# Reordering the first loads, pairing weight pieces in one buffer, and moving transposes at a stage seam, in a two-layer hybrid decoder trunk

## The chip, the cores and the metric

The kernel runs on one core of one Trainium2 chip. The metric is the device time of one execution in microseconds (us). PE is the matrix engine, DVE the vector engine, ACT the scalar (activation) engine, POOL the general-purpose engine; SP issues the DMA transfers. Every engine works through its own queue in order.

## The reference

Two layers over a sequence of 1024 tokens with 1024 features, float32. Each layer, cut to what matters:

```python
h = rms_norm(x, pre_mix_norm)
z = h @ w_in                       # 1024 -> 2*512 (conv) + 3*512 (q, k, v)
u = c_a * sigmoid(c_g)             # gated linear unit, 512 channels
u = silu(layer_norm(causal_dwconv(u, conv_w, conv_b)))      # 31 taps
q, k = partial_rope(zq), partial_rope(zk)                   # 4 heads, two 64-wide halves each
o = (softmax(q1 k1^T) - lam * softmax(q2 k2^T)) @ v         # causal
o = rms_norm(o, subln_g) * (1 - lam_init)
x = x + rms_norm(concat(u, o) @ w_out, post_mix_norm)
h = rms_norm(x, pre_ffn_norm)
up = causal_dwconv(h @ w_up, ffn_conv_w, ffn_conv_b)        # 1024 -> 2*2816, 3 taps
x = x + rms_norm((gelu(g) * val) @ w_down, post_ffn_norm)   # 2816 -> 1024
```

## The kernel before

**Precision and weights.** Every float32 operand of a matmul is split in two parts, hi and lo: ACT copies it into the reduced format (hi) and DVE or POOL subtracts to get the rest (lo). Each product is three matmuls, lo times lo being left out. A weight comes from DRAM into a tile `raw` (a ring of `RAW = 4` tiles of 1024 columns), is split into `wh..`/`wl..` tiles, and the raw tile is then free. In the mixing stage `load` cuts each weight into pieces of 512 columns (convolution weights, tag w) or 384 columns (query, key and value weights, tag q); each piece takes a whole raw tile. `split` does the ACT copy (L463) and the subtraction on POOL or DVE (L469). Tag w has two slots, tag q four.

**Start of layer 0.** Eight tiles of 128 tokens, here called t0 to t7, are loaded by `first_x` and normalised by `prenorm`: ACT squares and sums (L357), DVE scales the sum (L347), POOL takes the power -0.5 (L349), DVE multiplies (L359, the tile is then normalised in place), PE transposes eight blocks (L364) in two groups of four, ACT copies the hi part (L366) and DVE subtracts for lo (L367). The transposes of t4 to t7 are tied behind given products by `anchors`: with `CB[0] = (9, 0, 1, 2)` those of t4 are free, t5 follows the first convolution product (`pg`), t6 the second (`pa`), t7 the first product of queries, keys and values (`pq`). The raw tiles of the first convolution weights may be split only after the fourth power on POOL (`pows[3]`), those of the first q weights only after the eighth (`pows[7]`). Tiles for x come from two tags with two buffers each, "y" and "xr"; the order `("y", "y", "xr")[t % 3]` puts t0, t1, t3, t4, t6 and t7 in y. Before the loop the kernel also loads the causal mask `nmask` (cast on DVE at L262), `cos` and `sin`; behind it `params(0)` loads the convolution taps `cw`, `cvec`, `subg` and the lambda vectors and prepares them on DVE.

**Order of the mixing stage.** A planner, `Flow`, runs at build time over generators with assumed costs and due times; it writes out the order on PE, DVE, ACT and POOL (`manual_schedule`). It takes a raw ring slot with `R["raw"].get()` and assumes that a load takes `W_LAT = 3.0`. What is outside of the planner's blocks (the eight `prenorm`s, all SP transfers) is placed by the compiler's list scheduler. PE's fill is `c00 q00 c01 ...`: convolution product `pg` (gate) and `pa`, then four `pq` products of one head, and so on.

**The seam to the feed-forward stage.** Products of the up-projection are numbered by slots in `seq`; each slot is 12 matmuls of 128x512. The first sixteen slots compute two products for each of eight column tiles ahead: `(e1,1) (e1,4) (e2,1) (e2,4) (e1,7) ...`, where e2 adds into the PSUM tile `px` that e1 began, after `e_copy` (ACT, L1462) has copied e1's result out. Tokens t4 to t7 of the normalised input `xn` (L1185) are transposed here by `norm_t` (L1357) ahead of slots `NORM_T = (2, 5, 8, 11)`; `norm_c` then forms four sums of them on DVE and ACT at that slot and the three behind it. Slot 17 is the first that needs the sums (`t2`).

Of the kernel before, what the change touches and what calls it, by code (L numbers as in the profile page):

```python
# [9 lines left out]
F32 = mybir.dt.float32  # L10
# [42 lines left out]
P_AHEAD = 3  # L53
NORM_T = (2, 5, 8, 11)
ACC_BUFS = 3
# [158 lines left out]
def build(tc, ap, out):  # L214
# [7 lines left out]
    with ExitStack() as top:  # L222
# [17 lines left out]
        def load_x(src, tag="xr"):  # L240
            t = xs.tile([P, YW if tag == "y" else D], F32, tag=tag, name="xr", bufs=2 if tag == "y" else XR)[:, 0:D]
            sy.dma_start(t, src)
            return t
# [6 lines left out]
        xin = [ap["x"][t * P:(t + 1) * P, :] for t in range(8)]  # L250
        first_x = lambda t: load_x(xin[t], ("y", "y", "xr")[t % 3])
        x0 = [first_x(0)]
# [4 lines left out]
        g_pre = gvec(0, 0)  # L257
        x0 += [first_x(1), first_x(2)]
        nmask = xs.tile([P, P], F32, tag="m0", name="nmask", bufs=4)
        sy.dma_start(nmask, ap["nmask"])  # L260
        nmaskr = const("nmaskr", [P, P], mybir.dt.bfloat16)
        ve.tensor_copy(nmaskr, nmask)  # L262
        cos = const("cosT", [P, 8, 8])
        sy.dma_start(cos, ap["cos"])
        sin = const("sinT", [P, 8, 8])
        sy.dma_start(sin, ap["sin"])
        negh = const("negh", [P, 8])
        ve.memset(negh, -0.5)

        def params(l):  # L270
# [5 lines left out]

            cw, cv, sg = ptile("cw", [P, 4, CK]), ptile("cv", [P, 3, 4]), ptile("sg", [P, 1])
            sy.dma_start(cw, ap["cw"][l])
            sy.dma_start(cv, ap["cvec"][l])
            sy.dma_start(sg, ap["subg"][l])  # L280
            lv = par.tile([P, 4, HD], F32, tag="lv", name="lv", bufs=1)
            sy.dma_start(lv, ap["lamv"][l:l + 1].broadcast_to([P, 4, HD]))
            cws, hv, ls, nl = ptile("cws", [P, 4, (CK + 1) // 2]), ptile("hv", [P, 2, 4]), ptile("ls", [P, 2]), ptile("nl", [P, 1])
            pars[l] = dict(cw=cw, cws=cws, cv=cv, hv=hv, sg=sg, nl=nl)
            yield
# [128 lines left out]
        for l in range(DEPTH):  # L414
            xres = xin if l == 0 else x2[l - 1]
            with ExitStack() as st:
# [4 lines left out]
                if l == 0:  # L421
                    for t in range(8):
                        late[t] = prenorm(ptr, x0[t] if t < 3 else first_x(t), g_pre, hh[t // 4], t % 4)
                if l == 0:
                    for _ in params(0):
                        pass
                p = pars[l]
# [16 lines left out]
                def load(key, src, n, tag, gate=None):  # L444
# [8 lines left out]
                    W[key] = hi, lo, wi  # L453
                    step = n if n <= HB else n // 2
                    for j in range(n // step):
                        ri = yield from R["raw"].get()
                        raw = rw.tile([P, 1024], F32, tag="raw", name="raw", bufs=RAW)
                        s = slice(j * step, (j + 1) * step)
                        sy.dma_start(raw[:, :step], src[:, s])
                        fl.spawn(split(key, j, raw[:, :step], hi[:, s], lo[:, s], step, ri, gate), fl.now + W_LAT)  # L460

                def split(key, j, raw, hi, lo, n, ri, gate):
# [7 lines left out]
                    t = fl.op("dve", dv(n), t) if vec else fl.op("pool", 0.1 + n / 470, t)  # L470
                    R["raw"].free(ri, t)
                    fl.set("W", key, j)
# [797 lines left out]
                def next_params():  # L1270
                    g = params(l + 1)
                    yield 200.0
                    next(g)
                    yield 220.0
                    next(g, None)
                    fl.op("dve", 1.6)

                if l + 1 < DEPTH:
                    fl.spawn(next_params())
# [582 lines left out]
```

## Time and profile before

| what | us |
|---|---|
| median of 3 runs | 2315.07 |
| lowest, highest | 2315.03, 2316.55 |
| profiled execution, its own time | 2314.21 |
| span of its profile (first to last instruction) | 2312.4 |
| PE busy in the span | 2202.4 (95%) |
| DVE, ACT, POOL busy | 1879.3, 1126.7, 832.6 |
| mean granted TensorE clock | 0.979 of full speed |

The profiled execution is 0.9 us shorter than the median, and 1.8 us of its time lie outside of the span. A granted clock of 1.00 is 2.4 GHz and 0.5 is 1.2 GHz; a stretch with a clock between them was at the lower level for part of it. Times in rows count from the span's start.

### The profile page before, as it was taken

What the parts mean: (1) busy time and instruction counts of PE and PEld (TensorE: products, weight loads), DVE (VectorE), ACT (ScalarE), POOL (GpSimd) and SP (SyncE); (2) the same over time, 40 slices, a digit from 0 to 9 for tenths busy, and PEclk for the clock granted to TensorE, in tenths of its full rate; (3) what the DMA queues carried; (4) which work ended last, traced back from release to release, by engine and by line L of the source; (5) the groups of instructions that cost most, each with busy time, mean ns of one, the idle gap of its engine ahead of it and who ended that gap; (6) DMA issues with size and microseconds to landing.
All of it is one profiled execution on the core that took longest, in us unless ns stands there. A gap on an engine that the chain in (4) does not pass through costs nothing. (4 is left out here: it accounts for less than half of the span.)

```text
span 2312.4 us, 31516 instructions
## 1 busy us (share of the span) xinstructions
PE 2202.4 (95%) x10568; PEld 1838.5 (80%) x10568; DVE 1879.3 (81%) x3287; ACT 1126.7 (49%) x2458; POOL 832.6 (36%) x894
## 2 busy tenths in 40 slices
PE   6999997999999999999889999979999999999998
PEld 5898895878877878788778988868788778787886
DVE  6988988667888888777889889896678888887777
ACT  4445456655444444444534545465554444445443
POOL 3324312245444545201533333122454554442024
PEclk9999997999999999999999999979999999999999
DMA  4313323454333343933433123235533343348353
GB/s 156 86 48 92 79 72 123 164 206 138 119 120 130 111 137 130 316 96 111 135 100 103 41 82 97 73 114 191 194 118 124 119 136 123 104 168 274 96 164 118
DMA packets 140129, 295.39 MB, mean 128 GB/s; under 512 B 16832, under 2 KB 33984, under 8 KB 139456
## 3 DMA queue, kind: packets, MB, share of 16 engines
q1 hardware_dynamic: 139968, 293.39, 39.7%
q8 instruction: 83, 1.36, 0.3%
q14 instruction: 78, 0.64, 0.1%
HBM read 198.44 MB, written 78.12 MB: 120 GB/s over the span
## 5 line engine op out<-in xcount | busy, mean ns | idle before, releaser
L1660 PE MATMUL pd<-wp,wo 128*128 128x512 f32 x1776 | 414.2, 395 | 4.8 <-DVE wp L1305 2.8
L1660 PEld LDWEIGHTS pd<-wp,wo 128*128 128x128 f32 x1776 | 333.9, 188 | 81.7 <-DVE wp L1305 3.6
L1609 PE MATMUL py<-t,wo 128*128 128x512 f32 x1584 | 381.8, 394 | 5.8 <-DVE cg L1477 5.8
L1609 PEld LDWEIGHTS py<-t,wo 128*128 128x128 f32 x1584 | 296.8, 188 | 77.4 <-ACT wo L1304 9.0
L1305 POOL TENSOR_TENSOR wo<-ws,wo 128x512 fp32r<-128x512 f32 x176 | 249.9, 1432 | 279.5 <-ACT wo L1304 274.1
L1609 PE MATMUL px<-hA,wo 128*128 128x512 f32 x1056 | 255.3, 394 | 0.0
L1305 POOL TENSOR_TENSOR wo<-raw,wo 128x512 fp32r<-128x512 f32 x132 | 181.4, 1378 | 166.1 <-ACT wo L1304 157.3
L1609 PEld LDWEIGHTS px<-hA,wo 128*128 128x128 f32 x1056 | 198.6, 189 | 44.5 <-ACT ea L1464 0.5
L1305 POOL TENSOR_TENSOR wo<-fa,wo 128x512 fp32r<-128x512 f32 x66 | 103.1, 1577 | 323.0 <-ACT wo L1304 293.9
L1304 ACT ACTIVATE wo<-ws 128x512 fp32r<-128x512 f32 x176 | 108.8, 627 | 136.7 <-PE py L1609 47.4
L1495 DVE SCALAR_TENSOR_TENSOR acc<-cg,fw,acc 128x512 f32<-128x512 f32 x176 | 132.6, 754 | 41.7 <-ACT acc L1483 38.1
L597 DVE SCALAR_TENSOR_TENSOR scr<-u,cw,scr 128x256 f32<-128x256 f32 (+2 forms) x288 | 158.0, 565 | 3.7 <-ACT scr L591 3.6
L852 ACT ACTIVATE e<-S,mxv 128x512 f32<-128x512 f32 (+2 forms) x192 | 110.1, 581 | 64.6 <-DVE mxv L847 41.2
L1483 ACT ACTIVATE acc<-cg,fb,fw 128x512 f32<-128x512 f32 x88 | 68.2, 774 | 148.8 <-DVE cg L1477 148.8
L857 POOL TENSOR_TENSOR sm<-sm 128x1 f32<-128x1 f32 x64 | 25.5, 398 | 316.9 <-ACT e L852 301.6
L499 PE MATMUL pq<-whq,hA 128*128 128x384 f32 x512 | 135.5, 346 | 3.9 <-ACT whq L463 3.9
L499 PE MATMUL pq<-whq,hB 128*128 128x384 f32 x512 | 133.9, 342 | 0.0
L1609 PE MATMUL pz<-b,wo 128*128 128x512 f32 x528 | 129.8, 394 | 1.9 <-DVE cv L1477 1.9
L1609 PE MATMUL pz<-t,wo 128*128 128x512 f32 x528 | 128.7, 392 | 0.0
L1609 PEld LDWEIGHTS pz<-b,wo 128*128 128x128 f32 x528 | 98.4, 188 | 27.4 <-issue 5.1
L843 DVE TENSOR_REDUCE mxv<-S 128x1 f32<-128x512 f32 (+2 forms) x192 | 100.5, 549 | 24.1 <-PE S L827 18.2
L1609 PEld LDWEIGHTS pz<-t,wo 128*128 128x128 f32 x528 | 99.1, 188 | 22.7
(279 smaller groups left out, 5027.2 us busy)
## 6 DMA issues: line engine op xcount, KB each, us to landing
raw<-in_wupd SPq DMA_DIRECT2D x104, 512.0 KB, 3.6
fa<-f SPq DMA_DIRECT2D x154, 256.0 KB, 2.7
f<-fs SPq DMA_DIRECT2D x88, 256.0 KB, 3.3
raw<-in_wmix SPq DMA_DIRECT2D x80, 256.0 KB, 3.0
f<-gg SPq DMA_DIRECT2D x66, 256.0 KB, 2.0
raw<-in_wmix SPq DMA_DIRECT2D x64, 192.0 KB, 2.4
qs<-sth SPq DMA_DIRECT2D x64, 128.0 KB, 2.4
os<-onT SPq DMA_DIRECT2D x16, 512.0 KB, 3.2
```

Source lines behind the costliest of these rows:

```text
L499: mm = pe.matmul(dst, a, b, start=first and k + j == 0, stop=final and k == n - 1 and j == 2)
L597: ve.scalar_tensor_tensor(dst, src, wk, dst, op0=ALU.mult, op1=ALU.add)
L843: ve.tensor_reduce(mv_[:, j:j + 1], S, axis=AX.X, op=ALU.max, negate=True)
L852: se.activation(e[:, c0:c0 + w], S, AF.Exp, bias=mv_[:, 0:1], accum_out=sm[:, j:j + 1])
L857: po.tensor_tensor(sm[:, 0:1], sm[:, 0:1], sm[:, 1:2], op=ALU.add)
L1304: se.activation(w[:, 0], raw, AF.Copy)
L1305: eng.tensor_tensor(w[:, 1], raw, f32(w[:, 0]), op=ALU.subtract)
L1483: se.activation(acc[n, v, hf], C[n][v][:, 2 + hf * HB:2 + hf * HB + HB], AF.Identity, bias=fb[:, mt:mt + 1], scale=fw[:, mt, 2:3])
L1495: ve.scalar_tensor_tensor(dst, c[:, j + hf * HB:j + hf * HB + HB], fw[:, mt, j:j + 1], a, op0=ALU.mult, op1=ALU.add)
L1609: pe.matmul(ps, x, y, start=first and k + j == 0, stop=k == 3 and j == 2, skip_group_check=not first)
L1660: pe.matmul(ps[tt], x, y, start=first and k + n == 0, stop=k == K2 - 1 and n == 2, skip_group_check=not first)
```

## The change

Three edits. The start: the first four tiles of x (was three) are loaded ahead, over tags y, y, xr, xr in turn, and nothing but the identity and the norm's gain goes among them; `nmask`, `cos`, `sin` and the parameters of layer 0 are loaded by a task of the planner at its time 1.0, and the mask's cast and the parameters' preparation on DVE come at its time 7.0. `nmask` gets a tile of its own. The raw ring: one raw tile now takes all pieces of a weight, so the four tiles hold eight pieces; it is freed when the last piece is split. The seam: the transposes come ahead of slots 4, 6, 9 and 12.

```diff
-NORM_T = (2, 5, 8, 11)
+NORM_T = (4, 6, 9, 12)
...
-        first_x = lambda t: load_x(xin[t], ("y", "y", "xr")[t % 3])
+        first_x = lambda t: load_x(xin[t], ("y", "y", "xr", "xr")[t % 4])
         x0 = [first_x(0)]
...
         g_pre = gvec(0, 0)
-        x0 += [first_x(1), first_x(2)]
-        nmask = xs.tile([P, P], F32, tag="m0", name="nmask", bufs=4)
-        sy.dma_start(nmask, ap["nmask"])
+        x0 += [first_x(1), first_x(2), first_x(3)]
+        nmask = const("nmask", [P, P])
         nmaskr = const("nmaskr", [P, P], mybir.dt.bfloat16)
-        ve.tensor_copy(nmaskr, nmask)
         cos = const("cosT", [P, 8, 8])
-        sy.dma_start(cos, ap["cos"])
         sin = const("sinT", [P, 8, 8])
-        sy.dma_start(sin, ap["sin"])
...
             cw, cv, sg = ptile("cw", [P, 4, CK]), ptile("cv", [P, 3, 4]), ptile("sg", [P, 1])
+            lv = par.tile([P, 4, HD], F32, tag="lv", name="lv", bufs=1)
+            cws, hv, ls, nl = ptile("cws", [P, 4, (CK + 1) // 2]), ptile("hv", [P, 2, 4]), ptile("ls", [P, 2]), ptile("nl", [P, 1])
+            pars[l] = dict(cw=cw, cws=cws, cv=cv, hv=hv, sg=sg, nl=nl)
+            yield
             sy.dma_start(cw, ap["cw"][l])
             sy.dma_start(cv, ap["cvec"][l])
             sy.dma_start(sg, ap["subg"][l])
-            lv = par.tile([P, 4, HD], F32, tag="lv", name="lv", bufs=1)
             sy.dma_start(lv, ap["lamv"][l:l + 1].broadcast_to([P, 4, HD]))
-            cws, hv, ls, nl = ptile("cws", [P, 4, (CK + 1) // 2]), ptile("hv", [P, 2, 4]), ptile("ls", [P, 2]), ptile("nl", [P, 1])
-            pars[l] = dict(cw=cw, cws=cws, cv=cv, hv=hv, sg=sg, nl=nl)
             yield
...
-                        late[t] = prenorm(ptr, x0[t] if t < 3 else first_x(t), g_pre, hh[t // 4], t % 4)
+                        late[t] = prenorm(ptr, x0[t] if t < 4 else first_x(t), g_pre, hh[t // 4], t % 4)
                 if l == 0:
-                    for _ in params(0):
-                        pass
+                    par0 = params(0)
+                    next(par0)
...
                     step = n if n <= HB else n // 2
+                    ri = yield from R["raw"].get()
+                    raw = rw.tile([P, 1024], F32, tag="raw", name="raw", bufs=RAW)
                     for j in range(n // step):
-                        ri = yield from R["raw"].get()
-                        raw = rw.tile([P, 1024], F32, tag="raw", name="raw", bufs=RAW)
                         s = slice(j * step, (j + 1) * step)
-                        sy.dma_start(raw[:, :step], src[:, s])
-                        fl.spawn(split(key, j, raw[:, :step], hi[:, s], lo[:, s], step, ri, gate), fl.now + W_LAT)
+                        sy.dma_start(raw[:, s], src[:, s])
+                        fl.spawn(split(key, j, raw[:, s], hi[:, s], lo[:, s], step, ri if s.stop == n else None, gate), fl.now + W_LAT)
...
-                    R["raw"].free(ri, t)
+                    if ri is not None:
+                        R["raw"].free(ri, t)
...
                     yield 200.0
                     next(g)
+                    next(g)
                     yield 220.0
...
+                def constants():
+                    yield 1.0
+                    next(par0)
+                    sy.dma_start(cos, ap["cos"])
+                    sy.dma_start(sin, ap["sin"])
+                    sy.dma_start(nmask, ap["nmask"])
+                    yield 7.0
+                    next(par0, None)
+                    ve.tensor_copy(nmaskr, nmask)
+                    fl.op("dve", 1.8)
+
+                if l == 0:
+                    fl.spawn(constants())
```

## Rows read from the trace of the kernel before

**Rows 1.** The page: busy time of the engines, share of the span of 2312.4 us, and instructions.

```profile
PE 2202.4 (95%) x10568; PEld 1838.5 (80%) x10568; DVE 1879.3 (81%) x3287; ACT 1126.7 (49%) x2458; POOL 832.6 (36%) x894
```

**Rows 2.** Busy time by stretch: from and to, its length, then busy us and instructions of PE, PEld, DVE, ACT and POOL, the granted clock, the DMA share and GB/s.

```profile
340.00:410.00 70.00, 53.39 (x272) 43.31 (x270) 60.03 (x152) 41.33 (x117) 16.72 (x32) 0.83 0.40 121
1485.00:1555.00 70.00, 53.25 (x268) 42.38 (x267) 61.69 (x155) 40.90 (x117) 17.53 (x35) 0.78 0.35 105
```

**Rows 3.** The start in order of time: start, length, engine, line, operation, count, and in brackets the idle time of the engine before it with what ended it.

```profile
9.89 1.06 ACT L357 ACTIVATE sqj<-xr 128x1024 bf16<-128x1024 f32 x1 [4.44 <-DMA xr<-in_x]
11.16 1.06 ACT L357 ACTIVATE sqj<-xr 128x1024 bf16<-128x1024 f32 x1
11.37 0.23 DVE L262 CAST nmaskr<-nmask 128x128 bf16<-128x128 f32 x1 [6.62 <-DMA nmask<-in_nmask]
12.39 1.28 DVE L359 SCALAR_TENSOR_TENSOR xr<-xr,rs,gb 128x1024 f32<-128x1024 f32 x1 [0.73 <-POOL rs L349]
13.73 1.97 PE L364 MATMUL pt<-ident,xr 128*128 128x128 f32 x8 [13.73 <-DVE ss L347]
18.34 1.97 PE L364 MATMUL pt<-ident,xr 128*128 128x128 f32 x8 [2.65 <-DVE hA L367]
20.87 1.82 PE L364 MATMUL pt<-ident,xr 128*128 128x128 f32 x8 [0.56 <-DVE hA L367]
21.15 1.04 ACT L357 ACTIVATE sqj<-xr 128x1024 bf16<-128x1024 f32 x1
25.13 1.67 PE L364 MATMUL pt<-ident,xr 128*128 128x128 f32 x8 [2.44 <-DVE hA L367]
26.79 0.79 PE L499 MATMUL pg<-hA,whw 128*128 128x512 f32 x1
```

**Rows 4.** An issue of SP at the start; then one row of the list of issues (the last number is us from issue to landing), and one of what SP waited for up to 60 us (total, times, longest).

```profile
1.65 0.42 SPq L247 DMA_DIRECT2D gb<-in_norms  x1
gb<-in_norms SPq DMA_DIRECT2D x1, 512.0 KB, 6.9
SPq L459 <- POOL wlq L469: 14.6, 8, 6.9
```

**Rows 5.** The first product of q weights (PE from 43.48) and what feeds it, in order of time.

```profile
38.60 3.94 POOL L469 TENSOR_TENSOR wlq<-raw,whq 128x384 fp32r<-128x384 f32 x4 [1.23 <-ACT whq L463]
43.48 0.59 PE L499 MATMUL pq<-whq,hA 128*128 128x384 f32 x2
45.72 4.45 POOL L469 TENSOR_TENSOR wlq<-raw,whq 128x384 fp32r<-128x384 f32 x4 [3.17 <-ACT whq L463]
50.51 1.04 PE L364 MATMUL pt<-ident,xr 128*128 128x128 f32 x8
51.30 0.59 PE L499 MATMUL pq<-whq,hA 128*128 128x384 f32 x2
53.56 0.27 DVE L691 TENSOR_TENSOR v<-pq,v 128x128 fp32r<-128x128 f32 x1
55.54 0.51 PE L499 MATMUL pq<-whq,hA 128*128 128x384 f32 x2
```

**Rows 6.** A normalisation on DVE beside a split on POOL.

```profile
31.00 1.27 POOL L469 TENSOR_TENSOR wlw<-raw,whw 128x512 fp32r<-128x512 f32 x1
31.07 2.29 DVE L359 SCALAR_TENSOR_TENSOR xr<-xr,rs,gb 128x1024 f32<-128x1024 f32 x1 [2.07 <-POOL rs L349]
```

**Rows 7.** The same place at the start of layer 1.

```profile
1172.88 0.75 DVE L396 SCALAR_TENSOR_TENSOR y<-m0d,rs,xr 128x512 f32<-128x512 f32 x1 [1.68 <-POOL rs L349]
1179.69 0.59 PE L499 MATMUL pq<-whq,hA 128*128 128x384 f32 x2
1188.86 1.01 PE L499 MATMUL pq<-whq,hA 128*128 128x384 f32 x2 [3.92 <-ACT whq L463]
1190.25 1.46 DVE L396 SCALAR_TENSOR_TENSOR y<-m0d,rs,xr 128x512 f32<-128x512 f32 x1 [0.92 <-POOL wlq L469]
1194.52 1.91 PE L364 MATMUL pt<-ident,xr 128*128 128x128 f32 x8
1197.71 1.28 DVE L359 SCALAR_TENSOR_TENSOR xr<-y,rs,gb 128x1024 f32<-128x1024 f32 x1
1200.60 1.04 PE L364 MATMUL pt<-ident,xr 128*128 128x128 f32 x8
```

**Rows 8.** The seam of layer 0 in order of time; the last row is a stretch, as in rows 2.

```profile
505.77 1.28 DVE L1185 SCALAR_TENSOR_TENSOR xn<-xe,rs,gb 128x1024 f32<-128x1024 f32 x1
505.88 1.06 ACT L1178 ACTIVATE xn<-xe 128x1024 f32<-128x1024 f32 x1 [0.23 <-DVE ss L347]
506.94 0.58 ACT L1462 ACTIVATE ea<-px 128x512 f32<-128x512 f32 x1
507.19 1.94 PE L1357 MATMUL pt<-ident,xn 128*128 128x128 f32 x8 [3.88 <-DVE ss L347]
546.27 4.69 DVE L1372 TENSOR_TENSOR t<-ts,t 128x512 fp32r<-128x512 f32 x4
553.71 2.96 PE L1609 MATMUL py<-t,wo 128*128 128x512 f32 x12
500.00:520.00 20.00, 16.12 (x73) 13.31 (x72) 18.95 (x29) 13.35 (x25) 13.08 (x11) 0.91 0.71 257
```

**Rows 9.** The longest run of splits on POOL in the middle of the mixing stage of layer 0.

```profile
180.71 4.22 POOL L469 TENSOR_TENSOR wlq<-raw,whq 128x384 fp32r<-128x384 f32 x4
```

## The prediction

> **What bounds the kernel now.** I read the page first. PE is busy for 2202.4 of 2312.4 us [rows 1], so almost all of the time is matrix work that this change leaves alone; what it can win or lose lies in the 110 us in which PE stands, and in the time that PE works at its lower clock behind such a stand. The view by stretches says where these are. The two tails of the mixing stages, 70 us each, hold 16.6 and 16.8 us of standing, at a mean clock of 0.83 and 0.78 [rows 2]. Then I read PE's timeline for every gap over 0.3 us and the timelines of the engines that end them. The reader is to see three places outside of the tails. At the start PE's first transposes come at 13.73 and the first product at 26.79 [rows 3]. The first q product takes 7.0 us where the next takes 4.2 [rows 5], and its counterpart in layer 1 takes 14.8 [rows 7]. At the seam PE stands for 3.88 us ahead of the transposes [rows 8].
>
> **The start.** The first square on ACT is done long before DVE may scale it: the mask's cast stands ahead in DVE's queue and waits until 11.37, and 6.62 us of DVE's idle time end there. The first normalisation runs at 12.39 [rows 3]. Without the cast the next thing late is the gain: issued at 1.65, 6.9 us to landing, so 8.55 [rows 4]. The first normalisation may then run at about 8.7, which is 3.7 earlier, and the transposes at 10.0.
>
> Next is DVE's chain of four tiles. The fourth tile was late too (its square at 21.15), since its transfer waited for the transposes of the first. Now it is fourth in the queue and has a free buffer. The squares of the second and third tile began at 9.89 and 11.16 [rows 3]; one step more puts the fourth at about 12.4, and it binds no longer. Spacing of tiles on PE: 18.34 to 20.87 is 2.5 us with nothing late; 13.73 to 20.87 over two tiles is 3.6, but with the mask's successors, the parameters' small DVE instructions, between them [rows 3]. The last transposes would begin at 17.5 by the first and at 20.7 by the second. The first product came 1.66 behind them (25.13 to 26.79), so at 19.2 or 22.4 where it was at 26.79: a gain of 4.4 to 7.6. I take 5.5, near the middle, for splits on POOL now run beside this chain. A normalisation beside one took 2.29, against 1.28 [rows 3, 6].
>
> That row meets a rule that speaks against the change. The Trainium skill, page "SBUF — State Buffer", section "Who interferes with whom", says that a DVE instruction with two SBUF inputs and a GpSimd instruction that reads SBUF exclude each other, and that the later one waits out the earlier. The trace agrees here: 1.01 us of a 1.27 us split were added. If all four splits of the first weights met a normalisation, the rule would make the start up to 4 us worse and the sum below -5.4.
>
> The q product: its eight splits run in two groups, 38.60 to 42.5 and 45.72 to 50.2, and PE follows the second piece by piece [rows 5]. The second group is late because its raw tiles came free late: SP waited 14.6 us for these splits [rows 4]. With eight pieces in the ring, four of the eight are loaded at once and the rest as soon as the first convolution weights are split; in the planner's order all eight then come ahead of the convolution taps on ACT. The gate, the eighth power on POOL, comes with the tiles. The eight need 3.94 + 4.45 = 8.4 us on POOL and PE reaches them two products behind the start, so the 7.0 falls towards 4.2: a gain of 0 to 2.8. But DVE is full there. It frees the first product's PSUM bank at 53.8, and PE takes it again at 55.54 [rows 5], a slack of 1.7. DVE's lead stays at 5.5, so PE may gain 5.5 + 1.7 = 7.2 in all. Start: **-7.2**, bounds -4.4 and -10.4.
>
> The moved transfers (nmask, cos, sin and the four parameters, seven issues on SP) queue behind the first raw pieces and among the late x tiles, for whose buffers SP stands in its queue until PE has transposed the tile before. What needs them is late: the taps follow the second product, rope and the mask come later still. I cost them at nothing. If the order on DVE puts the preparation ahead of a late x tile, DVE waits for them as it now waits for the mask.
>
> **Layer 1.** The q product loses 14.8 - 4.2 = 10.6, from ACT's split standing behind taps that wait for DVE (3.92 of idle time) and from late pieces [rows 7]. The ring removes both. What is late next is DVE's chain for the last token tile: normalised at 1197.71, transposed at 1200.60. Its additions take 1.46 beside POOL's q splits (1190.25), where the same one of an earlier tile took 0.75 (1172.88); two tiles of two additions each run so, and with the q splits done before, 4 x 0.7 = 3 us come back. PE then waits for the transposes rather than for weights. Bounds 0 (the chain keeps its time) and -10.6; I take the chain: **-3.0**.
>
> **The seam.** PE stands until 507.19 because the first tile is normalised at 507.05. Moved two slots on, the transposes are not waited for. But slot 2, which PE reaches instead, adds into the bank that `e_copy` must have read, and that copy stands on ACT behind the four squares of the same normalisations: it runs from 506.94 to 507.52 [rows 8]. PE stands until about 507.6, then does the same work in another order. Slot 17 begins at 553.71, and DVE ends the sums of the last tile at 551.0 [rows 8], the one that slot 17 needs first among them: 2.7 us of cover for sums that start later, 0 if PE gains as much. So the stall only changes its name: +0.4 per layer, **+0.8** in all. The bounds: if ACT's order lets the copy run when its product is done, 3.88 goes, and with it the lower clock behind it. The stretch 500 to 520 has 0.91 [rows 8], that is 3.6 us at 1.2 GHz or 1.8 lost; 2 x 5.7 = -11.4. On the other side +3 if the sums come late.
>
> **The order of the rest.** The planner sees other load times and writes another order for 2 x 350 us of mixing. PE waits for no weights there now, so no gain is due; the tails, with 16 us of waits each [rows 2], can fall either way. I take 0, bounds -5 and +5.
>
> **Sum.** -7.2 - 3.0 + 0.8 + 0 = -9.4. Against the profiled 2314.2 that is 2304.8; the median lies 0.9 above it, so **2305.7**.
>
> **The rivals.**
> *The seam's stall does go.* For it: ACT idles between the squares, so an order with the copy among them exists. Against: nothing in the edit touches that order, and layer 1 has the same one. Time: the +0.8 becomes -11.4, so 2293.5.
> *The lead is eaten.* Constants that DVE waits for, splits beside normalisations, or taps on a DVE that is full leave only some 3 us of the start and nothing in layer 1, or the tails cost 5 more. For it: the start goes through DVE's queue tile by tile, and each of these would stand in that queue. Time: -3 to -4.4 + 0.8, so about 2312.
> *POOL's queue (slower).* A ring of eight pieces lets a whole q weight, eight splits, follow one another. The longest run in mid-stage is four, 4.22 us [rows 9]; eight would take 8.4, and the sums of the softmax, which POOL does between the exponentials and their combination, wait up to 4.2 more. There are three further q weights a layer, six places: 25 us if all is exposed on PE, so 2331. It decides (2319.7 and above) from (9.4 + 4.6) / 6 = 2.3 us exposed at each. Against: the four q slots come free one after another, so the loads stay spread, and PE has other products to fill with.
>
> **How the numbers follow.** 0.2% is 4.6 us; less than that a measurement of this kernel can't tell from no change. My sum, with 2299 to 2310.4 as its own range: 0.57. The seam's stall gone: 0.14. The lead eaten: 0.19. POOL's queue or another loss beyond 0.2%: 0.10. Faster takes the first two and a little of the third: 0.73; same 0.17; slower 0.10. The range takes in the second case and the third with the bounds of the terms that they share with mine, 2290 to 2316; it leaves out the slower case and the outer tenths of those two, some 0.17.
>
> **What would show it.** Right: DVE's first normalisation at 8.5 to 9, the first product at 19 to 22.5, the first q product about 4.2 us long, with its splits ahead of the taps; in layer 1 no wait for whq, and PE waiting for a normalisation instead; at the seam PE standing until 507.6 less the lead, released by the copy of L1462, with the transposes behind two products. Wrong: the copy ahead of the squares on ACT, or the first product still behind 24, or longer waits of PE in the tails than 16 us, released by POOL or by DVE's combination.

## The result: no gain, and a profile that gives the start's lead back

| | before | after |
|---|---|---|
| median, 16 runs each, same chip | 2315.05 | 2319.36 |
| lowest, highest | 2313.18, 2322.36 | 2317.21, 2321.33 |
| span of the profiled execution | 2312.4 | 2317.6 |

The ratio is 1.0016, with a 95% interval of 1.0009 to 1.0024: slower by 0.16%, which is within the 0.2% below which I said that a measurement can't tell it from no change. The forecast was 2305.7 with 0.73 for faster, and 2319.4 lies outside of its range of 2290 to 2316.

PE's busy time on the page of after, and the two tails by stretch (columns as in [rows 2]):

```profile
PE 2199.5 (95%) x10568; PEld 1837.2 (79%) x10568; DVE 1878.3 (81%) x3285; ACT 1127.9 (49%) x2458; POOL 831.0 (36%) x896
...
340.00:410.00 70.00, 54.36 (x276) 42.90 (x275) 63.36 (x161) 42.44 (x121) 19.68 (x35) 0.83 0.42 131
1485.00:1555.00 70.00, 52.71 (x286) 43.76 (x285) 63.01 (x164) 43.32 (x123) 17.45 (x34) 0.83 0.43 132
```

PE does the same work as in [rows 1] and stands 8 us longer. It is not the tails: they hold 15.6 and 17.3 us of standing, where [rows 2] had 16.6 and 16.8. To find the place I cut both profiles at the first instruction of certain products on PE; each entry is the length of that stretch in us.

| stretch on PE | before | after | difference |
|---|---|---|---|
| start to the first scores, layer 0 | 77.78 | 73.17 | -4.61 |
| first scores to the seam (mixing stage) | 419.93 | 424.04 | +4.11 |
| seam, first `px` to first `py` (slots 0 to 16) | 56.00 | 58.87 | +2.87 |
| rest of layer 0 | 612.40 | 612.28 | -0.12 |
| first product of layer 1 to its first scores | 57.63 | 55.97 | -1.66 |
| mixing stage, layer 1 | 421.07 | 422.93 | +1.86 |
| seam, layer 1 | 55.85 | 58.99 | +3.14 |
| rest of layer 1 | 611.74 | 611.35 | -0.39 |

The two starts gain 6.3, the two mixing stages lose 6.0, the two seams lose 6.0. The prediction had -10.2, 0 and +0.8 for these.

**The start of after**, the timeline of PE and DVE in order of time (columns as in [rows 3]):

```profile
9.13 1.97 PE L361 MATMUL pt<-ident,xr 128*128 128x128 f32 x8 [9.13 <-DVE xr L356]
...
13.10 1.28 DVE L356 SCALAR_TENSOR_TENSOR xr<-xr,rs,gb 128x1024 f32<-128x1024 f32 x1 [0.65 <-POOL rs L346]
14.30 1.28 DVE L364 TENSOR_TENSOR hA<-pt,hA 128x512 fp32r<-128x512 f32 x2
15.04 1.97 PE L361 MATMUL pt<-ident,xr 128*128 128x128 f32 x8 [3.94 <-DVE hA L364]
...
18.31 1.97 PE L361 MATMUL pt<-ident,xr 128*128 128x128 f32 x8 [1.30 <-DVE hA L364]
...
22.48 1.97 PE L361 MATMUL pt<-ident,xr 128*128 128x128 f32 x8 [2.21 <-DVE hA L364]
...
24.29 0.80 PE L497 MATMUL pg<-hA,whw 128*128 128x512 f32 x1
...
41.59 0.59 PE L497 MATMUL pq<-whq,hA 128*128 128x384 f32 x2
...
45.87 1.04 PE L361 MATMUL pt<-ident,xr 128*128 128x128 f32 x8
```

The first transposes come 4.6 us earlier than in [rows 3], the first product only 2.5. Between them PE waits three times for DVE's subtractions, which free the two PSUM tiles; the first of these, at 14.30, stands in DVE's queue behind the normalisation of the third tile at 13.10. The first q product takes 4.28 (41.59 to 45.87) where [rows 5] had 7.03.

**The rope of the second q product** (the rotation of q and k by position, six short instructions on DVE), the timeline of DVE, POOL and PE; first before, whose rows were not shown above:

```profile
100.55 2.04 POOL L469 TENSOR_TENSOR wlq<-raw,whq 128x384 fp32r<-128x384 f32 x2 [2.00 <-ACT whq L463]
...
101.64 1.10 DVE L710 TENSOR_TENSOR rp<-tok,sinT 128x128 f32<-128x128 f32 x1
102.66 0.28 DVE L709 TENSOR_TENSOR rp<-tok,cosT 128x128 f32<-128x128 f32 x1
102.75 1.07 POOL L469 TENSOR_TENSOR wlq<-raw,whq 128x384 fp32r<-128x384 f32 x1
102.86 1.10 DVE L710 TENSOR_TENSOR rp<-tok,sinT 128x128 f32<-128x128 f32 x1
...
104.55 0.88 PE L734 MATMUL ptq<-ident,tok 128*128 128x128 f32 x6 [0.56 <-DVE tok L712]
```

and after:

```profile
95.92 4.08 POOL L466 TENSOR_TENSOR wlq<-raw,whq 128x384 fp32r<-128x384 f32 x4 [2.00 <-ACT whq L460]
...
97.01 1.11 DVE L708 TENSOR_TENSOR rp<-tok,sinT 128x128 f32<-128x128 f32 x1
98.04 1.10 DVE L707 TENSOR_TENSOR rp<-tok,cosT 128x128 f32<-128x128 f32 x1
99.07 1.09 DVE L708 TENSOR_TENSOR rp<-tok,sinT 128x128 f32<-128x128 f32 x1
100.17 1.99 POOL L466 TENSOR_TENSOR wlq<-raw,whq 128x384 fp32r<-128x384 f32 x2
100.19 1.11 DVE L709 TENSOR_TENSOR tok<-rp,rp 128x128 f32<-128x128 f32 x1
101.22 1.07 DVE L710 TENSOR_TENSOR tok<-rp,rp 128x128 f32<-128x128 f32 x1
102.36 0.90 PE L732 MATMUL ptq<-ident,tok 128*128 128x128 f32 x3 [2.32 <-DVE tok L710]
```

The same DVE instruction takes 0.28 alone and 1.1 beside a split on POOL. In before two of the rope's six meet one, in after five do, because POOL now has six splits nearly in a row. PE's wait for the last of them grows from 0.56 to 2.32. That is the largest part of what PE loses in the middle: its stands of over 0.3 us in the first 250 us behind the first scores add up to 6.8 in before and to 9.7 in after.

**The seam of after**, the timeline of PE, DVE and ACT:

```profile
507.06 1.22 PE L1621 MATMUL px<-hA,wo 128*128 128x512 f32 x2 [4.25 <-ACT ea L1474]
...
516.15 0.69 DVE L1384 TENSOR_TENSOR ts<-pt,hA 128x512 f32<-128x512 f32 x1 [3.90 <-ACT ts L1386]
...
543.85 0.63 ACT L1316 ACTIVATE wo<-ws 128x512 fp32r<-128x512 f32 x1 [4.04 <-DVE ws L1432]
544.39 0.58 ACT L1476 ACTIVATE ea<-px 128x512 f32<-128x512 f32 x1
545.02 1.19 PE L1621 MATMUL px<-hA,wo 128*128 128x512 f32 x4 [1.65 <-ACT ea L1476]
```

The first stand is the renamed one of the prediction: 4.25, released by `e_copy`. DVE then idles for 3.90 until the transposes are copied, and begins its sums at 516.15; in before they began at 512.69, straight behind the normalisations. Near slot 13 there is a second stand of 1.65: the copy that PE needs is queued on ACT behind a split of a weight sum (`wo<-ws`), which waited 4.04 for DVE.

### The profile page after: what moved, and what is told of

Same layout as the page of the kernel before. It is cut to its first block, busy times and chain, and to the rows that moved or that the text cites. A ratio compares the mean times of both kernels' runs of the same rounds, so it can differ in the third digit from the quotient of the medians.

```text
span 2317.6 us, 31489 instructions
## 1 busy us (share of the span) xinstructions
PE 2199.5 (95%) x10568; PEld 1837.2 (79%) x10568; DVE 1878.3 (81%) x3285; ACT 1127.9 (49%) x2458; POOL 831.0 (36%) x896
## 5 line engine op out<-in xcount | busy, mean ns | idle before, releaser
L841 DVE TENSOR_REDUCE mxv<-S 128x1 f32<-128x512 f32 (+2 forms) x192 | 99.7, 548 | 16.7 <-PE S L825 15.6
```

What stands on the lines that cost most here:

```text
L841: ve.tensor_reduce(mv_[:, j:j + 1], S, axis=AX.X, op=ALU.max, negate=True)
```

## The experiments

All ratios are to runs of the kernel before on the same chip. Not all ran on one chip, so compare ratios and not medians. The stretches are those of the table above, and GpSimd in an expectation is POOL. A word on how far a stretch of one profile can be read: four kernels that have the same instructions up to the seam (before, and three experiments with the seam) took 419.2, 419.9, 422.1 and 422.5 us from the first scores to the seam. So a mixing stage is good to some 3 us. The same four took 75.6 to 77.8 from the start to the first scores, with before the slowest, so a start is good to some 2 us. A seam with the transposes where they were took 55.7 to 57.2, and once 58.4 (before_nolow below, layer 0, with a second stand of 2.50 for `e_copy`). The three kernels below with all of the pairing took 424.2 to 425.2 in the mixing stage of layer 0, after 424.0: that loss is above the scatter.

### The parts one by one

seam_alone is before with the third edit of the change, all_but_seam is after with that edit undone:

```diff
-NORM_T = (2, 5, 8, 11)
+NORM_T = (4, 6, 9, 12)
```

```diff
-NORM_T = (4, 6, 9, 12)
+NORM_T = (2, 5, 8, 11)
```

start_alone is before with the first edit (x tiles, constants and parameters), raw_alone before with the second, whose core is

```diff
+                    ri = yield from R["raw"].get()
+                    raw = rw.tile([P, 1024], F32, tag="raw", name="raw", bufs=RAW)
                     for j in range(n // step):
-                        ri = yield from R["raw"].get()
-                        raw = rw.tile([P, 1024], F32, tag="raw", name="raw", bufs=RAW)
```

> Kernel before with only NORM_T = (4, 6, 9, 12). Theory A (the seam itself costs): the profiles of before and after differ by 2.87 us between the first product of the seam and the first py product in layer 0 and by 3.14 in layer 1, so this edit alone makes the kernel about 6 us slower, ratio 1.0026, with PE standing about 4.3 us for the copy e_copy and some 1.6 us a second time near slot 15, also for e_copy. Rival B (the second stall comes only because the other two parts leave DVE late): PE stands once, the stall is renamed, +0.8 us, ratio 1.0003.

> Changed kernel with NORM_T back at (2, 5, 8, 11). Theory A: the 6.0 us of the two seams come back, about 2313.4 us, ratio to before 0.9993. Rival B: only 0.8 comes back and the loss lies in the mixing stages, about 2318.5, ratio 1.0015.

> Kernel before with only the moved constants and parameters and the fourth x tile ahead. First product at about 24.3 instead of 26.8, first q product still about 7 us long (late splits), so a lead of about 1.9 us when the first q product ends. Theory C (DVE sets the pace in the mixing stage, so a lead of PE alone is lost): no lead is left at the first product with the output weights (384.9 in before). Rival D (the lead stays, and what moves the mixing stage is only the order that the planner writes): the difference from there on is a scatter of either sign, up to 4 us a layer. Time by C 2315, by D anywhere from 2309 to 2319.

> Kernel before with only two pieces in a raw tile. The first product stays at 26.8; the first q product falls from 7.0 to about 4.3 us; in layer 1 the stretch from the first g product to the first transposes of q falls by about 1.7 us. Theory C: the 2.7 us lead is lost before the output product, total about 2314. Rival D: scatter of the mixing stage of either sign, 2307 to 2317. If POOL's burst of eight splits hurts, this kernel shows it alone: longer waits for POOL's sums in the mixing stage, over 2319.

| kernel | median | ratio | to first scores | mixing 0 | seam 0 | start of layer 1 | mixing 1 | seam 1 |
|---|---|---|---|---|---|---|---|---|
| seam_alone | 2319.32 | 1.0027 [1.0017, 1.0037] | -1.65 | +2.57 | +2.36 | +0.58 | -2.12 | +3.34 |
| all_but_seam | 2318.49 | 1.0012 [1.0003, 1.0021] | -3.94 | +4.39 | +0.90 | -0.06 | +2.09 | +1.18 |
| start_alone | 2316.18 | 1.0003 [0.9993, 1.0013] | +0.68 | +0.63 | -0.26 | 0.00 | +0.04 | -0.11 |
| raw_alone | 2318.64 | 1.0014 [1.0005, 1.0023] | -2.97 | +4.24 | +0.74 | -0.07 | +2.04 | +1.17 |

(Differences from before, in us.)

Theory A held for the seam alone: 0.27% slower, with both stands (4.25 and 1.93 in layer 0). It fell for what is left without the seam: 0.12% slower, not faster. The loss there is in raw_alone too, in the same stretches. So the pairing wins some 3 us at the start and loses more than that in the mixing stages; the moved constants alone win nothing that can be measured. start_alone missed its expectation: the first product came at 26.09 and not at 24.3, for the first transposes were at 10.36 (9.13 in after) and the parameters' preparation stood on DVE at 19.89, ahead of the subtraction that the fourth tile's transposes wait for. start_alone has the order of before on PE in every matmul, so only the pairing moved the planner. In both kernels with the pairing the seam takes about 1 us longer with the transposes where they were. The stand there is 3.88 as in before, but the lower clock behind it lasts longer (by stretch: from and to, length, busy us and matmuls of PE, granted clock, DMA share, GB/s; first before, from 2.2 us ahead of its transposes, then raw_alone, from 2.5 ahead):

```profile
505.00:513.00 8.00, 5.81 (x23) 0.79 0.46 186
```

```profile
506.00:514.00 8.00, 5.54 (x19) 0.57 0.51 207
```

8 us at a mean of 0.79 hold 3.4 us at 1.2 GHz, at 0.57 they hold 6.9. That the pairing brings this about is not shown: the seam of layer 0 in pair_first_only and both seams of q_on_dve (below), which load one piece per tile there, have the longer stretch too and take 57.0, 56.9 and 57.2. Two things stay open. The parts add up to +0.44%, with some 0.17% of uncertainty, and the whole is +0.16%; in the same way the seam's edit costs 0.27% alone, but undoing it in after wins only 0.04%, though the two seams of that profile are 3.9 us shorter. And the 1.66 us that after gains at the start of layer 1 are in none of the other kernels with all of its pairing (raw_alone, all_but_seam and, below, ws_early).

### What the pairing loses in the mixing stage

One edit on raw_alone (raw_nolow) and on before (before_nolow), which leaves out the low halves of the q weights:

```diff
-                    (ve if vec else po).tensor_tensor(lo, raw, f32(hi), op=ALU.subtract)
+                    if key[0] == "q":
+                        po.memset(f32(lo), 0.0)
+                    else:
+                        (ve if vec else po).tensor_tensor(lo, raw, f32(hi), op=ALU.subtract)
```

> raw_alone, but GpSimd's subtraction for the q weights is replaced by a memset of the low halves: it reads nothing, and the low halves of the q weights are left out of the result. The order of all engines stays that of raw_alone. Theory L (a run of GpSimd's splits holds up DVE's small instructions of the rope, each of which then takes 1.1 us instead of 0.28, and PE's transposes behind them stand 2.32 us at about 104): the eight rope instructions fall from 7.3 us to about 2.4, PE's wait falls to under 0.6, and PE's idle time between 60 and 330 falls from 10.0 us towards the 6.9 of before. Rival M (the new order of the planner is the cause, with any duration on DVE): the wait of PE stays at over 1.5 us.

> The kernel before with the same memset in place of the subtraction for the q weights (low halves left out). Theory L: the two rope instructions that take 1.10 us at 101.64 and 102.86 fall to 0.28, PE's 0.56 us at 104.55 go, and raw_nolow is from the first scores on no slower than this kernel. Rival M: raw_nolow still stands some 3 us more between 60 and 330 than this kernel.

(There are six rope instructions, not eight; in raw_alone they take 5.85 us, not 7.3.) Measured: 2298.83, ratio 0.9935 [0.9920, 0.9950], and 2299.15, ratio 0.9933 [0.9920, 0.9947]. The rope of raw_nolow on DVE, PE behind it, and a later place on POOL and DVE:

```profile
95.99 0.28 DVE L714 TENSOR_TENSOR rp<-tok,sinT 128x128 f32<-128x128 f32 x1
...
99.65 0.61 PE L738 MATMUL ptq<-ident,tok 128*128 128x128 f32 x4
...
257.34 1.49 POOL L470 MEMSET wlq<- 128x384 f32 x4
257.52 0.29 DVE L714 TENSOR_TENSOR rp<-tok,sinT 128x128 f32<-128x128 f32 x1
```

All six are short, and PE waits no longer. No memset ran beside these six; the last two rows are a place where one did. In the whole profile 18 instructions of the rope ran beside a memset, and each took 0.28 or 0.29. PE's busy time between 60 and 330 (columns as in the two stretches of the seam above) in before, raw_alone, before_nolow and raw_nolow, in this order:

```profile
60.00:330.00 270.00, 263.13 (x1524) 0.99 0.27 75
```

```profile
60.00:330.00 270.00, 259.98 (x1508) 0.99 0.25 72
```

```profile
60.00:330.00 270.00, 266.64 (x1561) 0.99 0.27 75
```

```profile
60.00:330.00 270.00, 266.54 (x1571) 1.00 0.26 74
```

With subtractions on POOL the pairing costs 3.2 us of PE in this stretch; with memsets, in the same two orders on PE, 0.1. (Without the edit every kernel with all of the pairing has 259.8 to 260.0 here; before, start_alone and the three with the seam's experiments have 263.1 to 263.6.) Over the whole mixing stage of layer 0 the four take 419.9, 424.2, 415.1 and 415.1: the 4.2 that the pairing loses are gone, and both kernels gain besides. Theory L stands and M falls. What the memset also takes away is POOL's time (0.4 for one, about 1.0 for a subtraction), so the figure is for both; the lengths of DVE's instructions, beside a split and beside a memset, show the hold-up by itself.

The Trainium skill has this as a rule: page "SBUF — State Buffer", section "Who interferes with whom", where a DVE instruction with two SBUF inputs and a GpSimd (POOL) instruction that reads SBUF exclude each other. The trace agrees, 0.28 against 1.1, and the memset, which reads nothing, held up none of the 18. The prediction weighed that rule at the start alone.

q_on_dve, on before:

```diff
-                    vec = key[0] == "w" and td < tp
+                    vec = key[0] == "q" or key[0] == "w" and td < tp
```

> Kernel before with the subtraction of all q splits on DVE instead of GpSimd (the planner counts their time, about 0.47 us each, 32 in a layer). If the hold-up of DVE by GpSimd's reads costs more than the work itself, this is faster: DVE's two-input instructions fall back to their short times, up to 0.5 us saved at each split that met one, 2305 us, ratio 0.996. If DVE's time is what counts, 15 us more work a layer on an engine that is busy nine tenths of the mixing stage makes it slower: 2325 us, ratio 1.005.

Measured: 2345.23, ratio 1.0133 [1.0119, 1.0146], 30 us slower. The stretches 60 to 330 and 330 to 400 of this kernel (length, then busy us of PE, PEld, DVE, ACT and POOL, granted clock, DMA share, GB/s):

```profile
60.00:330.00 270.00, 267.88 (x1570) 243.24 (x1569) 230.47 (x542) 130.97 (x399) 51.59 (x97) 1.00 0.26 73
330.00:400.00 70.00, 47.75 (x233) 39.02 (x231) 64.28 (x173) 37.90 (x114) 15.98 (x35) 0.70 0.35 102
```

Up to 330 this is the fullest PE of all kernels, 267.88 of 270. Then the tail takes it back and more, with PE down to 47.75 (before 55.15) and the clock at 0.70. The mixing stages took 435.2 and 435.9 us, 15.3 and 14.9 more than before. (My expectation counted the layer's 15 us and then wrote a time that holds less than both layers.) That this is near the 15 us of the expectation is luck: 24 of a layer's 32 splits fall in the stage, at 0.55 each some 13 us, but DVE's other instructions got shorter, and its busy time in the stage rose by only 5.6 and 3.6 us (345.6 and 345.4 in before, 351.2 and 349.0 here). Its idle time rose by 9.6 and 11.2. The planner counted the splits on DVE and wrote another order for PE as well, from just behind the first scores. What of the loss is DVE's added work, what the order and what the lower clock of the tail, is not shown; the run shows only that freeing DVE of the hold-up in this way does not pay.

### The pairing where it pays

pair_first, on all_but_seam:

```diff
-                    ri = yield from R["raw"].get()
-                    raw = rw.tile([P, 1024], F32, tag="raw", name="raw", bufs=RAW)
+                    pair = key in (("c", 0, 0), ("c", 0, 1)) or key[:-1] == RUN["q", 0, 0]
                     for j in range(n // step):
+                        if j == 0 or not pair:
+                            ri = yield from R["raw"].get()
+                            raw = rw.tile([P, 1024], F32, tag="raw", name="raw", bufs=RAW)
...
```

pair_first_three_x, on pair_first:

```diff
-        first_x = lambda t: load_x(xin[t], ("y", "y", "xr", "xr")[t % 4])
+        first_x = lambda t: load_x(xin[t], ("y", "y", "xr")[t % 3])
...
-        x0 += [first_x(1), first_x(2), first_x(3)]
+        x0 += [first_x(1), first_x(2)]
...
-                        late[t] = prenorm(ptr, x0[t] if t < 4 else first_x(t), g_pre, hh[t // 4], t % 4)
+                        late[t] = prenorm(ptr, x0[t] if t < 3 else first_x(t), g_pre, hh[t // 4], t % 4)
```

pair_first_only is before with pair_first's way of loading, and the constants where they were.

> The changed kernel with NORM_T back at (2, 5, 8, 11) and two pieces in a raw tile for the first two weights of the convolution and the first q weight of a layer alone; all other loads as in before. Theory L (the lead of the start is lost because the pairing makes GpSimd's splits of the later q weights run in a row beside the rope): the lead of about 4 us at the first scores (77.8 in before) is kept behind the first rope (PE waits 0.56 there and not 2.32) and at the seam's first product; 2311 us or less, ratio 0.9980 to 0.9985. Theory C (DVE is full in the mixing stage, so that a lead of PE there is lost whatever the splits do): the lead is gone by the seam's first product, ratio 1.000.

> pair_first with three x tiles ahead instead of four. Theory G (with four tiles ahead ACT does the squares of the third and fourth before it copies the first tile's transposes, which then free the banks late: 15.04 for the second transposes where the first came at 9.13): the second transposes come at 13.7 or before and the first product at 23 or before. Rival H (the fourth tile's own lateness is worse): the second transposes come earlier but the fourth come behind 23, and the first product at 24.5 or later.

> Kernel before with two pieces in a raw tile for the first two weights of the convolution and the first q weight alone; constants and parameters loaded as in before. The order on PE is that of pair_first. If the moved constants are worth what the two starts show together (4.6 us with both, 3.0 with the pairing alone at the first scores), 3 us are gained at the first scores and kept: 2312 us, ratio 0.9987. If the moved constants are worth nothing, as start_alone showed (0.7 lost at the first scores), the same as pair_first: 0.9974.

| kernel | median | ratio | to first scores | mixing 0 | seam 0 | start of layer 1 | mixing 1 | seam 1 |
|---|---|---|---|---|---|---|---|---|
| pair_first | 2309.69 | 0.9974 [0.9963, 0.9985] | -6.61 | -0.41 | -0.11 | +0.37 | -0.75 | +0.13 |
| pair_first_three_x | 2310.03 | 0.9973 [0.9963, 0.9983] | -6.21 | +2.15 | +0.01 | +0.13 | -0.21 | +0.18 |
| pair_first_only | 2311.03 | 0.9982 [0.9973, 0.9991] | -4.09 | +0.55 | +1.02 | +1.07 | -0.67 | +0.15 |

pair_first beats both kernels. In its profile the lead of the start goes through the mixing stage, and the wait behind the rope is that of before:

```profile
97.92 0.55 PE L735 MATMUL ptq<-ident,tok 128*128 128x128 f32 x3 [0.56 <-DVE tok L713]
```

So Theory C, that a lead is lost in the mixing stage whatever the splits do, falls, in so far as DVE has the lead as well (its first normalisation ran at 7.64, in before at 12.39). This profile is of an execution 3.2 us below the median; pair_first_ws below, with the same instructions up to the seam, has a lead of 4.01 at the first scores and loses 1.53 of it in the mixing stage. The ratio is what shows that a lead is kept. How much of it is the moved constants' stays open: 0.9974 with them, 0.9982 without, and the intervals overlap; the pairing of the first weights alone has two thirds of the gain.

Theory G falls too, as to the second transposes. With three tiles ahead ACT copies the first transposes at 10.81 (12.76 in after), and yet, in the timeline of ACT, DVE and PE of pair_first_three_x:

```profile
8.62 1.97 PE L361 MATMUL pt<-ident,xr 128*128 128x128 f32 x8 [8.62 <-DVE xr L356]
...
10.81 1.06 ACT L363 ACTIVATE hA<-pt 128x512 fp32r<-128x512 f32 x2
12.48 1.28 DVE L356 SCALAR_TENSOR_TENSOR xr<-xr,rs,gb 128x1024 f32<-128x1024 f32 x1 [0.65 <-POOL rs L346]
13.68 1.28 DVE L364 TENSOR_TENSOR hA<-pt,hA 128x512 fp32r<-128x512 f32 x2
14.42 1.97 PE L361 MATMUL pt<-ident,xr 128*128 128x128 f32 x8 [3.83 <-DVE hA L364]
```

DVE's queue has three normalisations ahead of the first subtraction, and the spacing of the first two transposes is 5.80 as in after (5.91). The first product came at 22.26, within the 23 of Theory G and 1.7 earlier than in pair_first, but the first q product no earlier (39.99 and 39.59).

### The seam

norm3_alone, on before:

```diff
-NORM_T = (2, 5, 8, 11)
+NORM_T = (3, 5, 8, 11)
```

three_e1 is that and three early products ahead (the third and the last of them in the bank of pO):

```diff
-seq = [(j, n) for q in range(0, len(early), 2) for j in ("e1", "e2") for n in early[q:q + 2]]
+seq = [(j, n) for q in (slice(0, 3), slice(3, 5), slice(5, 8)) for j in ("e1", "e2") for n in early[q]]
...
-px[n] = (pmm.tile([P, HB], F32, tag="mm", name="px") if j == "e1" else
+px[n] = (pmm.tile([P, HB], F32, tag="mm", name="px") if j == "e1" and n not in (early[2], early[7]) else
```

ws_early, on after, issues the two weight sums that slot 17 needs two slots earlier on DVE:

```diff
+                    at(slot[6, 0] - WO_BUFS - 1, lambda: wsums(0, 1, 2), True)
```

pair_first_ws is pair_first with this line; pair_first_three_e1_ws has the order of three_e1 besides.

> Kernel before with NORM_T = (3, 5, 8, 11): only the first tile's transposes move, and by one product. Theory A2 (PE stands for e_copy either way; what the change loses beyond that is that DVE's sums begin 3.5 us later, as the transposes wait behind two products, and DVE sets the pace up to slot 17): the first sum on DVE begins within 0.7 us of before's 512.69 (as measured from the seam's first product), PE stands about 4.25 us for e_copy once and not a second time, the seam takes 56.0 to 56.7 us (before 55.9, with both products moved 58.4 to 59.2), ratio 1.0004. Rival E (each product of delay costs its share): seam about 57.4, ratio 1.0013.

> Kernel before with NORM_T = (3, 5, 8, 11) and three early products ahead instead of two (the third in the bank of pO; groups of 3, 2 and 3 early products). Theory A2: PE works until about 506.1 (from 497.7) and stands 1.1 to 1.5 us instead of 3.88, the lower clock behind it is shorter or gone, DVE keeps its times and its last sums end at about 551 (before's times); the seam is 2 to 2.7 us shorter in each layer, 2310 us, ratio 0.9980. Rival F (DVE's chain sets the first py product wherever PE stands): PE stands later instead, just ahead of slot 17, and the seam stays at 55.5 or more, ratio 0.9998.

> The changed kernel, with the two sums of weights on DVE for slot 17 issued two slots earlier (ahead of the third tile's sums); the order on PE, ACT and GpSimd is untouched. Theory A3 (the second stall of 1.65 us comes from ACT, where the split of these sums waits for DVE and e_copy stands behind it): the split no longer waits some 4 us for DVE, the second stall is gone in both layers, and the seam takes 57 us instead of 58.9; 2316 us, ratio to before 1.0004, if nothing else is late by then. Rival F (DVE as a whole is late, and PE needs its last sums at slot 17): the second stall goes, but PE stands about as long ahead of slot 17, ratio 1.0016.

> pair_first (transposes at the seam as in before) with the two weight sums for slot 17 issued two slots earlier on DVE. Theory A3 (in before's order the copy e_copy behind these sums is done just as PE needs it, so nothing is to be won there): seam 55.9 us as in before, ratio 0.9974 as pair_first. Rival: DVE, with the sums out of the way, ends the last tile's sums earlier and the seam shortens by up to 1 us in each layer, ratio 0.9966.

> pair_first with three early products ahead, NORM_T = (3, 5, 8, 11), and the two weight sums two slots earlier. Theory F (DVE's sums, one tile behind the other without a pause, set when slot 17 can begin; a stand of PE ahead of that costs nothing by itself): the first stand is 1.2 us instead of 3.88, but PE stands later for DVE or for the copies behind DVE, and the seam takes 55 us or more; ratio 0.997 or above. Rival I (three_e1 lost only by the two stalls of 1.81 and 4.41 us for e_copy behind the weight sums): with the sums earlier both go and the seam takes 53.2 us, ratio 0.9952.

| kernel | median | ratio | seam 0 | seam 1 | PE's stands over 0.8 us in the seam of layer 0 |
|---|---|---|---|---|---|
| norm3_alone | 2320.89 | 1.0027 [1.0019, 1.0036] | 58.40 | 61.39 | 4.26 and 1.92, both for `e_copy` |
| three_e1 | 2323.96 | 1.0040 [1.0028, 1.0053] | 61.30 | 61.02 | 1.17 for DVE, 1.81 and 4.41 for `e_copy` |
| ws_early | 2317.95 | 1.0012 [1.0003, 1.0021] | 56.40 | 57.32 | 4.25 for `e_copy` |
| pair_first_ws | 2310.90 | 0.9974 [0.9965, 0.9984] | 55.90 | 55.68 | 3.88 for DVE |
| pair_first_three_e1_ws | 2320.14 | 1.0023 [1.0014, 1.0032] | 61.66 | 61.53 | 1.16 for DVE, 0.87 and 6.57 for `e_copy` |

ws_early shows the second stand's cause. The split no longer waits, and the copy begins 44.3 us behind the seam's first product (499.92), in after 47.2 behind it (497.21). PE's second stand is gone in both layers (ACT):

```profile
543.71 0.62 ACT L1316 ACTIVATE wo<-ws 128x512 fp32r<-128x512 f32 x1
544.23 0.57 ACT L1477 ACTIVATE ea<-px 128x512 f32<-128x512 f32 x1
```

The seams fell by 2.5 and 1.7; the total by 0.04%, less than it can be told from.

norm3_alone refutes Theory A2 as I put it. DVE's first sum began at 513.14, only 0.45 later than in before, and still both stands came. On the way DVE lost two waits for ACT (0.76 and 0.50) and met POOL's splits elsewhere (an addition of 1.66 where before had 0.69), and was 2.4 us late at the weight sums. In before the copy near slot 13 ended at 542.6, which is when PE reached the slot that needs it (12 matmuls of 0.23 behind 539.83): that seam has no slack at all.

The two with three early products show where the next limit is. PE's first stand fell from 3.88 to 1.17, as hoped, and nothing was won: PE stood later, for `e_copy` behind a split that waits for a weight sum on DVE, which is done when DVE has come that far. The timeline of three_e1:

```profile
545.62 4.67 DVE L1372 TENSOR_TENSOR t<-ts,t 128x512 fp32r<-128x512 f32 x4
...
550.22 0.68 DVE L1420 TENSOR_TENSOR ws<-raw,ws 128x512 f32<-128x512 f32 x1
550.99 0.63 ACT L1304 ACTIVATE wo<-ws 128x512 fp32r<-128x512 f32 x1 [3.61 <-DVE ws L1420]
551.52 0.58 ACT L1464 ACTIVATE ea<-px 128x512 f32<-128x512 f32 x1
552.16 1.22 PE L1609 MATMUL px<-hA,wo 128*128 128x512 f32 x2 [4.41 <-ACT ea L1464]
```

From the seam's first product to the end of DVE's last sums it is 54.2 us here and 53.3 in before [rows 8]. Between the first sum and the last DVE is idle for 0.5 of 39.2 us here and for 1.3 of 38.3 in before: it is full whether PE stands early or late. Taking the first weight sums out of the way moved the wait to the next weight sum (6.57). Whether a seam in which no copy stands behind a weight sum would be shorter is not shown.

## Why the prediction was wrong

**The start: -7.2 forecast, -4.6 measured** (good to some 2). The first normalisation (8.7 forecast, 7.79 measured) and the first transposes (10.0, 9.13) came as forecast or earlier, but the first product won 2.5 where 5.5 were forecast. The step that failed is the spacing of the tiles: 2.5 to 3.6 us forecast, 5.9, 3.3 and 4.2 measured. [Rows 3] had the better figure, 11.4 us over the three pairs. I had left out the last pair as late, and had taken the first for disturbed by the parameters; but its 4.6 was DVE's order, and that did not change. The q product fell to 4.28, as forecast (5.66 in raw_alone, 7.20 in start_alone). start_alone moved the first scores by +0.7: the gain there comes with the pairing.

**Layer 1: -3.0 forecast, -1.7 measured, and 0 in its relatives.** The mechanism was half right. The wait for `whq` is gone, the last tile's two additions are short again (0.75 where [rows 7] has 1.46), and the last tile's transposes come 30.3 us behind the layer's first product, 34.5 in before. The step that failed is the four times 0.7: the other tile's two additions still stand beside the splits (1.29 and 1.50 at 1181.89 and 1183.11). Then PE waits 2.31 for DVE's addition to v, and POOL's row of six splits delays two powers, for which DVE stands 2.54 (timeline of POOL and DVE of after):

```profile
1181.57 6.78 POOL L466 TENSOR_TENSOR wlq<-raw,whq 128x384 fp32r<-128x384 f32 x6 [1.26 <-ACT whq L460]
...
1188.90 1.28 DVE L356 SCALAR_TENSOR_TENSOR xr<-y,rs,gb 128x1024 f32<-128x1024 f32 x1 [2.54 <-POOL rs L346]
```

**The seam: +0.8 forecast, +6.0 measured.** The renamed stand was right to 0.03 us: +0.37 in a layer, +0.4 forecast. The failed step is the cover: I took 2.7 us, between DVE's last sums and slot 17. What is late first is not slot 17 but `e_copy` near slot 13, which stands on ACT behind work that waits for DVE, and its cover is nothing. The bound of +3, "if the sums come late", had the direction; measured was about that in each layer.

**The order of the rest: 0 forecast, +6.0 measured.** This step failed by leaving out a term. That PE waits for no weights in the middle was true, and said nothing: the splits cost there by standing beside DVE, as raw_nolow shows: the 3.2 us that the pairing takes from PE between 60 and 330 go with them. The rival of POOL's queue had the row of splits, gave it 0.10, and made POOL's sums its victim; the victim was DVE, first of all the rope of the second q product, at 1.76 us on PE in each layer. The row that showed it (an instruction beside a split, [rows 6]) was on the table, used for the start alone.

**The sum.** -6.3 + 6.0 + 6.0 - 0.5 for the rest is +5.2 between the two profiles, +4.3 between the medians.

## What to carry to other kernels

When a change lets transfers or splits come in longer runs, look for the instructions of another engine that will stand beside the run, and price them by a row in which the two already meet, at every place and not only where the change aims. Before a stand on one engine is moved, find the engine that is full through that stretch (in the seam DVE, idle for 1.3 of 38.3 us): when PE's first stand went from 3.88 to 1.17 there, PE stood later instead. The cover of a delay is the slack of the first thing that becomes late, and that may be a small copy queued behind something else.

## What was unexpected in the hardware

A DVE instruction of 0.28 us takes 1.1 beside a subtraction of 1.0 on POOL, and one of 1.28 takes 2.29 beside one of 1.27 [rows 6]. In these rows each meeting adds 0.8 to 1.0 us, whatever the instruction's own length, so by them a row of splits costs most where many short instructions stand beside it. The lower clock adds its own noise to profiles: in seam_alone 35 us of the mixing stage with the order and busy time of before ran at a mean clock of 0.95 and not 1.00 (first before),

```profile
190.00:225.00 35.00, 31.68 (x182) 1.00 0.35 106
```

```profile
190.00:225.00 35.00, 31.70 (x172) 0.95 0.32 94
```

which is 3.5 us at 1.2 GHz, or 1.7 us of time, in one execution and not in the other.
